# Layer 0 gate and up projection: seven block products for eight on four channel tiles, in a written instruction order

## The chip, the core and the metric

One of the eight cores of a Trainium2 chip runs the whole program: TensorE (PE; its weight loads are listed as PEld), VectorE (DVE), ScalarE (ACT), GpSimd (POOL) and SyncE (SP), which issues the DMAs. The metric is the device time of one execution in microseconds. The kernel before took 3100.1 us (median of 3 runs, 3099.51 to 3101.63).

## What is computed

Two layers of a backbone over 256 latent tokens (`h`) and 256 context tokens (`hc`), 2048 channels, fp32 throughout. Layer 0 mixes tokens by pooling, layer 1 by neighbourhood attention, and each is followed by a gated MLP with 5504 hidden channels. The part that the change touches is the MLP of layer 0, for both streams, and the modulation vectors of layer 1, which are computed beside it:

```python
def conv_ffn(u, w_gate, w_up, conv_w, conv_b, w_down):
    T = u.shape[1]
    gp = jnp.pad(u @ w_gate, ((0, 0), (1, 1), (0, 0)))
    gte = gp[:, :T] * conv_w[0] + gp[:, 1:T + 1] * conv_w[1] + gp[:, 2:] * conv_w[2] + conv_b
    return (jax.nn.silu(gte) * (u @ w_up)) @ w_down
...
ml = (silu_c @ w_mod[i] + b_mod[i]).reshape(B, 6, 1, D)
...
h = h + ml[:, 5] * conv_ffn(modulate(rms_norm(h, norm2_g[i]), ml[:, 3], ml[:, 4]),
                            ffn_w_gate[i], ffn_w_up[i], ffn_conv_w[i], ffn_conv_b[i], ffn_w_down[i])
...
hc = hc + mc[5] * conv_ffn(modulate(rms_norm(hc, norm2_g[i]), mc[3], mc[4]), ...)
```

## The kernel before, in words

Channels lie on the 128 partitions, so 2048 channels are 16 channel tiles (`KT`), and the 5504 hidden channels are 43 hidden tiles `f` (`NF`). The normalised input of the MLP stands in 16 tiles `A[k]`, each `[128, 2, 2, 256]`: first index high and low part, second the stream (latent, context), third the token. Every fp32 number is split into a high part that TensorE multiplies in one pass (type fp32r) and the rest, its low part; a product is three matmuls (weight high by input high, weight high by input low, weight low by input high), accumulated in a PSUM bank.

`load` fetches weights in pieces of 128 x 1024 (512 KB), `split` makes the two halves: ScalarE copies the high part (line 143), VectorE subtracts it to give the low part (line 145). In the MLP of layer 0 the pairs of high and low tiles come from four buffers in turn (three of the pool `whp`, one of `whx`), each 1024 columns wide.

- `gu0(f)` computes gate and up for hidden tile `f`: for each of the two, 16 channel tiles by three matmuls over 512 columns (both streams side by side), lines 631 to 633, so 96 matmuls per hidden tile. The first eight hidden tiles come from another place (`partial`, before the stage).
- `gate0` makes the activation of a hidden tile: the centred convolution (lines 364, 366, 368), SiLU (371), the product with up (372) and the split into high and low (378, 379).
- `down0(c, ...)` takes a chunk of four hidden tiles to the 16 output tiles (`mg`, `m`): lines 657 to 659, 12 matmuls for one output tile, 192 for a chunk of four. Of every chunk but the last ScalarE multiplies the bank by the modulation gate (line 669, two streams) and GpSimd adds the result to `hl` or `hc` (line 670). For the last chunk VectorE does both in one operation from PSUM (line 663).
- `mod_pairs` computes the modulation of layer 1 beside this on VectorE: for pieces of `wmod`, fetched into a ring of three staging buffers two steps ahead, a multiply-add by a scalar into `macc` (lines 239 and 241), at the end of a vector a transposition and a sum (251, 252), a small matmul (`quarter_sum`) and the bias (181). It is a generator, `pump`: each `next(pump)` is one piece, and calls in `gu0` and `down0` place them.

The order of the whole program is set by a scheduler over the instructions of all engines; it may move instructions of one engine past each other. Staging buffers (`wst`) are three for weights and three for the modulation in this stage.

## Time and profile before

| | |
|---|---|
| median of 3 runs | 3100.1 us |
| the profiled execution | 3103.48 us, of which its span 3101.7 us |
| PE busy | 3030.0 us (98%), 15082 instructions |
| DVE busy | 1932.6 us (62%), 2748 instructions |
| ACT busy | 1373.2 us (44%), 2219 instructions |
| POOL busy | 826.1 us (27%), 823 instructions |
| chain that ended last | PE 94% |

The stage of the MLP of layer 0 with full hidden tiles lies between about 520 and 1710 us of the span. Times of the profile are counted from the span's start. A line such as "L631 PE MATMUL g<-A,wg" names line, engine, operation, what is written and what is read. Matmuls are pipelined: a matmul over 512 columns is listed with some 390 ns, and the next one starts long before it ends, so that the cost of one is the distance from start to start.

### The profile page before, as it was taken

How to read it: one execution, taken by the hardware profiler on the slowest of the kernel's cores; microseconds unless marked ns; L12 is line 12 of the kernel's file. 1: busy time of each engine (PE TensorE's matmuls, PEld its weight loads, DVE VectorE, ACT ScalarE, POOL GpSimd, SP SyncE). 2: the span in 40 equal slices, each digit the busy share in tenths (PEclk: the TensorE clock that was granted, in tenths of full speed). 3: DMA queues.
4: the chain of work that ended last, by engine and by line, in shares of the span. 5: the costliest groups of instructions: out<-in, count | busy, mean ns of one | idle time of the engine just before them, and what ended most of it. 6: DMA issues, size and time to landing. Idle time of an engine off the chain costs nothing.

```text
span 3101.7 us, 40819 instructions
## 1 busy us (share of the span) xinstructions
PE 3030.0 (98%) x15082; PEld 2414.3 (78%) x15082; DVE 1932.6 (62%) x2748; ACT 1373.2 (44%) x2219; POOL 826.1 (27%) x823
## 2 busy tenths in 40 slices
PE   6999899999999999999999999999999999999998
PEld 2565558888888888888888788878788888888887
DVE  4445674285765848567485665564777666666666
ACT  3333454333233332323334444343545666656665
POOL 2011213213031230302213000000002466556665
PEclk9999999999999999999999999999999999999999
DMA  9978573264846657475573333332345565555563
GB/s 376 333 271 306 177 246 102 89 217 149 251 141 206 198 162 247 133 225 171 182 226 118 102 113 106 102 114 96 111 153 179 177 196 188 192 189 185 179 195 117
DMA packets 177927, 559.70 MB, mean 180 GB/s; under 512 B 17600, under 2 KB 22208, under 8 KB 177728
## 3 DMA queue, kind: packets, MB, share of 16 engines
q1 hardware_dynamic: 177728, 557.10, 55.0%
q8 instruction: 119, 1.95, 0.3%
q14 instruction: 80, 0.66, 0.1%
HBM read 554.93 MB, written 2.10 MB: 180 GB/s over the span
## 4 chain that ended last, share of the span: by engine, by line
PE 94%; DMA 2%; DVE 2%; POOL 1%; ACT 1%; issue 0%; SPq 0%; DVEq 0%; ACTq 0%; POOLq 0%
PE g L766 5%; PE u L766 5%; PE d L657 5%; PE d L659 5%; PE d L658 5%; PE d L813 4%; PE u L631 4%; PE u L632 4%; PE u L633 4%; PE g L631 4%; PE g L633 4%; PE g L632 4%; PE mod L193 3%; PE u L769 3%; PE g L769 3%; PE d L817 2%
## 5 line engine op out<-in xcount | busy, mean ns | idle before, releaser
L670 POOL TENSOR_TENSOR hl<-hl,dy 128x256 f32<-128x256 f32 x160 | 149.0, 931 | 958.6 <-ACT dy L669 957.3
L828 POOL TENSOR_TENSOR hl<-hl,dy 128x256 f32<-128x256 f32 x320 | 331.5, 1069 | 188.4 <-ACT dy L826 186.1
L241 DVE SCALAR_TENSOR_TENSOR macc<-wm,sc,macc 128x512 f32<-128x512 f32 (+1 forms) x360 | 325.2, 935 | 68.6 <-DMA wm<-wmod 67.6
L669 ACT ACTIVATE dy<-d,modT 128x256 f32<-128x256 f32 x320 | 133.5, 470 | 196.8 <-PE d L659 195.5
L193 PE MATMUL mod<-wm,sc 128*32 128x512 f32 x768 | 134.6, 618 | 26.6 <-DMA wm<-wmod 26.5
L670 POOL TENSOR_TENSOR hc<-hc,dy 128x256 f32<-128x256 f32 x160 | 126.0, 787 | 0.0
L145 DVE TENSOR_TENSOR wd_2l<-wd,wd_2h 128x1024 fp32r<-128x1024 f32 (+1 forms) x44 | 53.9, 1229 | 112.8 <-ACT wd_2h L143 112.8
L826 ACT ACTIVATE dy<-d,modT 128x512 f32<-128x512 f32 x160 | 104.4, 683 | 42.7 <-PE d L817 41.2
L915 POOL TENSOR_TENSOR rk<-rk,rp 128x256 f32<-128x256 f32 x16 | 13.2, 826 | 365.4 <-DVE rk L914 309.8
L145 DVE TENSOR_TENSOR wd_3l<-wd,wd_3h 128x1024 fp32r<-128x1024 f32 (+1 forms) x44 | 52.0, 1202 | 80.6 <-ACT wd_3h L143 80.6
L145 DVE TENSOR_TENSOR wd_1l<-wd,wd_1h 128x1024 fp32r<-128x1024 f32 (+1 forms) x44 | 53.7, 1224 | 58.6 <-ACT wd_1h L143 58.6
L466 POOL TENSOR_TENSOR pf<-ws,inv 128x256 f32<-128x256 f32 x32 | 27.7, 886 | 222.4 <-DVE ws L461 154.7
L193 PEld LDWEIGHTS mod<-wm,sc 128*32 128x32 f32 x768 | 23.6, 110 | 81.0 <-issue 59.4
L143 ACT CAST wd_1h<-wd 128x1024 fp32r<-128x1024 f32 (+1 forms) x44 | 45.2, 1029 | 79.8 <-PE u L632 50.6
L145 DVE TENSOR_TENSOR wd_0l<-wd,wd_0h 128x1024 fp32r<-128x1024 f32 (+1 forms) x44 | 54.6, 1247 | 40.7 <-ACT wd_0h L143 40.6
L1004 ACT ACTIVATE sb<-sb,nm 128x512 f32<-128x512 f32 x64 | 46.1, 721 | 64.4 <-DVE nm L1000 63.2
L143 ACT CAST wd_0h<-wd 128x1024 fp32r<-128x1024 f32 (+1 forms) x44 | 45.3, 1031 | 57.9 <-PE u L766 29.1
L792 DVE TENSOR_TENSOR actb<-sgb,actb 128x256 fp32r<-128x256 f32 x43 | 52.3, 1216 | 27.0 <-ACT actb L791 27.0
L657 PE MATMUL d<-act,wd_2h 128*128 128x512 f32 x172 | 68.0, 395 | 0.0
L658 PE MATMUL d<-act,wd_2h 128*128 128x512 f32 x172 | 67.9, 395 | 0.0
L657 PE MATMUL d<-act,wd_3h 128*128 128x512 f32 x172 | 67.9, 395 | 0.0
L657 PE MATMUL d<-act,wd_0h 128*128 128x512 f32 x172 | 67.9, 395 | 0.0
(1752 smaller groups left out, 9286.1 us busy)
## 6 DMA issues: line engine op xcount, KB each, us to landing
wm<-wmod SPq DMA_DIRECT2D x384, 512.0 KB, 6.1
wd<-wd SPq DMA_DIRECT2D x168, 512.0 KB, 4.4
wg<-wg SPq DMA_DIRECT2D x156, 512.0 KB, 4.6
wu<-wu SPq DMA_DIRECT2D x156, 512.0 KB, 4.5
wv<-wv SPq DMA_DIRECT2D x32, 512.0 KB, 3.9
wk<-wq SPq DMA_DIRECT2D x32, 512.0 KB, 4.0
wq<-wq SPq DMA_DIRECT2D x32, 512.0 KB, 3.7
wo<-wo SPq DMA_DIRECT2D x32, 512.0 KB, 4.4
```

The lines of the kernel that those rows point to most:

```text
L145: eng.tensor_tensor(lo[:, :n], t[:, :n], hi[:, :n].bitcast(F32), op=ALU.subtract)
L193: nc.tensor.matmul(ps[32 * j : 32 * j + 32, :], sc[:, 4 * g + j, :], ts[j // 2][0][:, 512 * (j % 2) : 512 * (j % 2) + 512], start=(g == 0) ...
L241: nc.vector.scalar_tensor_tensor(acc[s], v, sc2[:, k, s : s + 1], acc[s], op0=ALU.mult, op1=ALU.add)
L631: nc.tensor.matmul(ps, hi[:, c : c + P], xh, start=(k == 0), stop=False)
L632: nc.tensor.matmul(ps, hi[:, c : c + P], xl, start=False, stop=False)
L633: nc.tensor.matmul(ps, lo[:, c : c + P], xh, start=False, stop=(k == KT - 1))
L657: nc.tensor.matmul(ps, hi[:, o : o + P], xh, start=(i == 0), stop=False)
L658: nc.tensor.matmul(ps, hi[:, o : o + P], xl, start=False, stop=False)
L670: nc.gpsimd.tensor_tensor(h_of(s)[:, k, :], h_of(s)[:, k, :], y[:, s], op=ALU.add)
L766: nc.tensor.matmul(ps, hi[:, c : c + P], flat(B[k]), start=(k == 0), stop=False)
L769: nc.tensor.matmul(ps[:, T:], lo[:, c : c + P], B[k][:, 0], start=False, stop=(k == KT - 1))
L828: nc.gpsimd.tensor_tensor(hl[:, k, :], hl[:, k, :], y[:, q], op=ALU.add)
```

## The change

From the second chunk (`down(1)`) to the last gate and up (hidden tile 42), the stage is written as a list of `works` (matmul groups), `units` (splits of a weight, now 512 columns of high and 512 of low in one buffer), `loads` and `gates` (small steps of an activation), and emitted in that order inside `tc.manual_schedule`, which leaves the instructions of the five engines in the order written. The last chunk is still done by `down0`, under the scheduler.

Channel tiles 0 to 3 of gate and up are done by Strassen's method: the two streams by two halves of the four channel tiles form one 2 x 2 block matrix, the two halves by gate and up the other, and seven products of 256 columns (two channel tiles each) take the place of eight. Sums of the inputs (`sums`) are made once; sums of the weights (`first`, `second`) and of the products (`lacks`) are made by GpSimd in each hidden tile, and VectorE adds them to the banks (`fix`). The result of a chunk's down projection is added to the streams by VectorE alone, straight from PSUM. The chunks become `runs` (the third has three hidden tiles, the last four). The modulation gives up control after each half of a piece, and says how long it took, and the loop calls it by a running account (`due`) that grows by 0.40 of the matmul time.

```diff
-            for k, v in loaded[i]:
+            for j, (k, v) in enumerate(loaded[i]):
+                if j:
+                    yield 1.6
...
+            yield 1.4 if m == 2 else 1.6
...
-            yield
-        ending()
...
+    runs = [[*range(4)], [*range(4, 8)], [8, 9, 10]] + [list(range(f, f + 4)) for f in range(11, NF, 4)]
...
-        extra.append(whx)
...
-                if c > 1:
-                    next(pump, None)
...
+        J = 2
+        JC = P * J
...
+        NR = NW // 2
+        SLOTS = 7
+        def half(v, n, name):
...
+            hi, lo = t[:, :n], t[:, 512 : 512 + n]
+            nc.scalar.copy(hi, v)
+            nc.vector.tensor_tensor(lo, v, hi.bitcast(F32), op=ALU.subtract)
...
+            def fix():
+                for ps, e in ((b1, e1), (b2, e2)):
+                    nc.vector.tensor_tensor(ps, ps, flat(e), op=ALU.add)
...
+            def first():
+                b11, b12, b22 = x.t[:, :JC], y.t[:, :JC], y.t[:, JC : 2 * JC]
+                z = box["z"] = whx.tile([P, 2 * JC], F32, tag="z", bufs=2, name=nm + "z")
+                nc.gpsimd.tensor_tensor(z[:, :JC], b12, b11, op=ALU.subtract)
+                nc.gpsimd.tensor_tensor(b12, b22, b12, op=ALU.subtract)
+                nc.gpsimd.tensor_tensor(z[:, JC:], b22, z[:, :JC], op=ALU.subtract)
+
+            def second():
+                nc.gpsimd.tensor_tensor(x.t[:, :JC], x.t[:, JC : 2 * JC], box["z"][:, JC:], op=ALU.subtract)
...
+                        nc.tensor.matmul(ps, hi[:, c : c + P], xh, start=(own and i == 0), stop=False)
+                        nc.tensor.matmul(ps, hi[:, c : c + P], xl, start=False, stop=False)
+                        nc.tensor.matmul(ps, lo[:, c : c + P], xh, start=False, stop=(own and i == J - 1))
...
+            def lacks():
+
+                e1, e2 = box["e1s"], box["e2s"]
+                nc.gpsimd.tensor_tensor(e2[:, 0], e2[:, 0], e1[:, 0], op=ALU.add)
+                nc.gpsimd.tensor_tensor(e1[:, 1], e1[:, 1], e2[:, 0], op=ALU.add)
+                nc.gpsimd.tensor_tensor(e2[:, 0], e2[:, 0], e2[:, 1], op=ALU.add)
+                nc.gpsimd.tensor_tensor(e2[:, 1], e2[:, 1], e1[:, 1], op=ALU.add)
...
+            wide, small = 0.69, 0.35
+            work([g1], wide * R, others(g1, "b1", 2 * J, R, True, False), [g1])
+            work([u1], wide * R, others(u1, "b2", 2 * J, R, True, False), [u1])
+            work([w0], small * J, product(1, w0, 0, "e1", 0))
+            work([w0], small * J, product(2, w0, 1, "b1", 0), [w0])
+            work([w1], small * J, product(7, w1, 0, "e1", 1), [], out("e1"))
+            work([w1], small * J, product(3, w1, 1, "b2", 0), [w1])
+            work([w2], small * J, product(6, w2, 1, "e2", 0))
+            work([w2], small * J, product(5, w2, 0, "e2", 1), [w2], out("e2"))
+            work([w3], small * J, product(4, w3, 0, "b1", 1), [w3])
+            work([g2], 4 * wide, others(g2, "b1", 8, 4, False, False), [g2], lacks)
...
+                    def end(m=m, mg=mg, ps_=ps_):
+                        k = 4 * mg + m
+                        for s in both:
+                            nc.vector.scalar_tensor_tensor(h_of(s)[:, k, :], ps_[m][:, T * s : T * s + T], M(0, 5, k, s),
+                                                           h_of(s)[:, k, :], op0=ALU.mult, op1=ALU.add)
...
+        gates.extend(sums(0) + sums(1))
+        down(1)
+        for c, fs in enumerate(runs):
+            for i, f in enumerate(fs):
+                if f > NS:
+                    tile0(f)
+                    if i == 0 and c > 2:
+                        down(c - 1)
+
+        with tc.manual_schedule(engines={mybir.EngineType.PE, mybir.EngineType.Activation, mybir.EngineType.DVE,
+                                         mybir.EngineType.Pool, mybir.EngineType.SP}):
...
+                if started:
+                    due = min(due + 0.40 * us, 6.0)
+                if more_:
+                    for _ in range(2):
+                        if due > 0:
+                            due -= next(pump, 1.0e9)
```

What this does to the order. On PE, at the start of hidden tile 20, the kernel before has (`g0_20` is the bank, `A0_0_3` channel tile 0):

```order
L631 MATMUL g0_20_6868<-A0_0_3_2896,wg0_20h0_6839 128x512
L632 MATMUL g0_20_6868<-A0_0_3_2896,wg0_20h0_6839 128x512
L633 MATMUL g0_20_6868<-A0_0_3_2896,wg0_20l0_6840 128x512
L631 MATMUL g0_20_6868<-A1_0_3_2936,wg0_20h0_6839 128x512
L632 MATMUL g0_20_6868<-A1_0_3_2936,wg0_20h0_6839 128x512
```

and the change, after 24 such matmuls on channel tiles 4 to 7 (`e1` is a bank of its own, `b1` that of the gate, `s3` an input sum):

```order
L886 MATMUL w0_20_b1_7679<-A2_0_3_2985,w0_20_b1_7590 128x256
L887 MATMUL w0_20_b1_7679<-A2_0_3_2985,w0_20_b1_7590 128x256
L888 MATMUL w0_20_b1_7679<-A2_0_3_2985,w0_20_b1_7590 128x256
L886 MATMUL w0_20_b1_7679<-A3_0_3_3048,w0_20_b1_7590 128x256
L887 MATMUL w0_20_b1_7679<-A3_0_3_3048,w0_20_b1_7590 128x256
L888 MATMUL w0_20_b1_7679<-A3_0_3_3048,w0_20_b1_7590 128x256
L886 MATMUL w0_20_e1_7729<-s3_0_4120,w0_20_b2_7651 128x256
L887 MATMUL w0_20_e1_7729<-s3_0_4120,w0_20_b2_7651 128x256
L888 MATMUL w0_20_e1_7729<-s3_0_4120,w0_20_b2_7651 128x256
```

The 24 matmuls of 512 columns on channel tiles 0 to 3 are gone; 42 of 256 columns stand there.

On DVE, in the first quarter of a down projection (chunk or run 5), the kernel before has splits of weights and one activation, no adding to the streams:

```order
L145 TENSOR_TENSOR wd0_5_0l0_8467<-wd0_5_0_0_8462,wd0_5_0h0_8466 128x1024
L145 TENSOR_TENSOR wd0_5_0l1_8471<-wd0_5_0_1024_8464,wd0_5_0h1_8470 128x1024
L366 SCALAR_TENSOR_TENSOR g1_27_8452<-g0_27_8333,vt_70,g1_27_8452 128x2x255
L368 SCALAR_TENSOR_TENSOR g1_27_8452<-g0_27_8333,vt_70,g1_27_8452 128x2x255
L145 TENSOR_TENSOR wd0_5_1l0_8557<-wd0_5_1_0_8552,wd0_5_1h0_8556 128x1024
```

and the change (`macc` is the modulation, `hl` and `hc` the streams, `w0_23` and `act_23` hidden tile 23):

```order
L252 SCALAR_TENSOR_TENSOR macc_1_3_8103<-wm1_3_5_8319,sc2_81,macc_1_3_8103 128x512 x2
L804 SCALAR_TENSOR_TENSOR g1_23_8493<-w0_23_b1_8279,vt_70,g1_23_8493 128x2x255
L806 SCALAR_TENSOR_TENSOR g1_23_8493<-w0_23_b1_8279,vt_70,g1_23_8493 128x2x255
L947 SCALAR_TENSOR_TENSOR hl_84<-d0_5_0_0_8489,modT0_20_3075,hl_84 128x256
L947 SCALAR_TENSOR_TENSOR hc_91<-d0_5_0_0_8489,modT0_20_3075,hc_91 128x256
L814 TENSOR_TENSOR sg_23_8503<-sg_23_8503,w0_23_b2_8301 128x512
L252 SCALAR_TENSOR_TENSOR macc_1_3_8103<-wm1_3_5_8319,sc2_81,macc_1_3_8103 128x512 x2
L822 TENSOR_TENSOR act_23_8517<-sg_23_8503,act_23_8517 128x512
L947 SCALAR_TENSOR_TENSOR hl_84<-d0_5_0_1_8513,modT0_20_3075,hl_84 128x256
L947 SCALAR_TENSOR_TENSOR hc_91<-d0_5_0_1_8513,modT0_20_3075,hc_91 128x256
```

Modulation, activation and the adding to the streams now stand in one queue between the splits.

On POOL the adds to the streams are gone from these runs, and each hidden tile has eight sums, four of weights (lines 838 to 843, with the next tile's ahead) and four of products (900 to 903):

```order
L843 TENSOR_TENSOR w0_20_x_7480<-w0_20_x_7480,w0_20_z_7569 128x256
L838 TENSOR_TENSOR w0_21_z_7750<-w0_21_y_7695,w0_21_x_7669 128x256
L839 TENSOR_TENSOR w0_21_y_7695<-w0_21_y_7695 128x256
L840 TENSOR_TENSOR w0_21_z_7750<-w0_21_y_7695,w0_21_z_7750 128x256
L900 TENSOR_TENSOR w0_20_e2s_7784<-w0_20_e2s_7784,w0_20_e1s_7760 128x256
L901 TENSOR_TENSOR w0_20_e1s_7760<-w0_20_e1s_7760,w0_20_e2s_7784 128x256
L902 TENSOR_TENSOR w0_20_e2s_7784<-w0_20_e2s_7784 128x256
L903 TENSOR_TENSOR w0_20_e2s_7784<-w0_20_e2s_7784,w0_20_e1s_7760 128x256
```

Over the written part this makes, on DVE, 446 splits of 512 columns and 34 of 256, 288 adds to the streams of 128 x 256, 68 `fix` adds of 128 x 512, and the unchanged activations and modulation; on POOL 272 sums for the 34 hidden tiles and 12 for the inputs (four of 512 columns, eight of 256).

## Rows read from the trace of the kernel before

**Rows 1.** The page: the chain that ended last, by engine.

```profile
PE 94%; DMA 2%; DVE 2%; POOL 1%; ACT 1%; issue 0%; SPq 0%; DVEq 0%; ACTq 0%; POOLq 0%
```

**Rows 2.** Busy us by stretch: length, PE, PEld, DVE, ACT, POOL, then PE clock, DMA share, GB/s.

```profile
520.00:1650.00 1130.00, 1130.00 (x4942) 925.25 (x4941) 716.62 (x884) 388.80 (x582) 228.74 (x275) 1.00 0.59 185
2380.00:3060.00 680.00, 680.00 (x3894) 597.21 (x3893) 454.27 (x461) 419.58 (x612) 410.73 (x339) 1.00 0.58 188
```

**Rows 3.** Line 631, gate matmuls: duration ns min/median/max, first and last start us.

```profile
L631 PE MATMUL g<-A,wg_9h x16: 389/389/397, 521.2 to 531.4; 128*128 128x512 f32 x16
...
L631 PE MATMUL g<-A,wg_11h x16: 389/389/389, 565.1 to 575.3; 128*128 128x512 f32 x16
```

**Rows 4.** Timeline of PE (start us, us): a down projection's first matmul, and two gate stretches.

```profile
852.59 0.40 PE L657 MATMUL d<-act,wd_0h 128*128 128x512 f32 x1
...
897.12 0.40 PE L631 MATMUL g<-A,wg_20h 128*128 128x512 f32 x1
...
899.66 0.39 PE L631 MATMUL g<-A,wg_20h 128*128 128x512 f32 x1
...
908.29 0.40 PE L633 MATMUL g<-A,wg_20l 128*128 128x512 f32 x1
```

**Rows 5.** Timeline of PE in layer 1's last chunk: 256 columns, 36 matmuls apart.

```profile
3069.60 0.28 PE L809 MATMUL d<-actb,wd_0h 128*128 128x256 f32 x1
...
3073.92 0.28 PE L809 MATMUL d<-actb,wd_1h 128*128 128x256 f32 x1
```

**Rows 6.** Line 809, its weight loads: duration ns min/median/max.

```profile
L809 PEld LDWEIGHTS d<-actb,wd_0h x12: 192/192/192, 3069.5 to 3073.4; 128*128 128x128 f32 x12
```

**Rows 7.** Groups by line and shape, 520 to 1650 us: count | busy us, mean ns | idle before.

```profile
L241 DVE SCALAR_TENSOR_TENSOR macc<-wm,sc,macc 128x512 f32<-128x512 f32 x240 | 171.3, 761 | 0.2
L241 DVE SCALAR_TENSOR_TENSOR macc<-wm,sc,macc 128x1024 f32<-128x1024 f32 x120 | 153.9, 1282 | 68.4 <-DMA wm<-wmod 67.6
L366 DVE SCALAR_TENSOR_TENSOR g<-g,vt,g 128x510 f32<-128x510 f32 x35 | 26.1, 745 | 0.5
L372 DVE TENSOR_TENSOR sg<-sg,u 128x512 f32<-128x512 f32 x35 | 23.9, 683 | 34.4 <-PE u L633 33.6 <-ACT sg L371 0.8
L251 DVE STREAM_TRANSPOSE modu<-macc 128x512 f32<-128x512 f32 x30 | 19.5, 688 | 0.0
L252 DVE TENSOR_REDUCE modr<-modu 128x16 f32<-128x512 f32 x30 | 18.6, 660 | 0.0
L239 DVE TENSOR_SCALAR macc<-wm,sc 128x512 f32<-128x512 f32 x16 | 8.9, 598 | 0.0
L143 ACT CAST wd_0h<-wd 128x1024 fp32r<-128x1024 f32 x18 | 18.9, 1051 | 27.3 <-PE g L632 27.3
```

**Rows 8.** Lines 379, 663, 670 and 792: duration ns min/median/max.

```profile
L379 DVE TENSOR_TENSOR act<-sg,act x43: 678/685/1270, 420.9 to 1635.4; 128x512 fp32r<-128x512 f32 x43
L663 DVE SCALAR_TENSOR_TENSOR hl<-d,modT,hl x16: 474/482/485, 1675.8 to 1707.5; 128x256 f32<-128x256 f32 x16
L670 POOL TENSOR_TENSOR hl<-hl,dy x160: 729/738/1682, 480.7 to 1674.4; 128x256 f32<-128x256 f32 x160
L792 DVE TENSOR_TENSOR actb<-sgb,actb x43: 418/427/2432, 2388.5 to 3057.0; 128x256 fp32r<-128x256 f32 x43
```

**Rows 9.** Timeline: two operations back to back on DVE; a DVE and a POOL operation at once.

```profile
1024.70 1.40 DVE L241 SCALAR_TENSOR_TENSOR macc<-wm,sc,macc 128x512 f32<-128x512 f32 x2
...
864.84 1.23 DVE L145 TENSOR_TENSOR wd_2l<-wd,wd_2h 128x1024 fp32r<-128x1024 f32 x1 [0.18 <-ACT wd_2h L143]
...
865.32 1.34 POOL L670 TENSOR_TENSOR hl<-hl,dy 128x256 f32<-128x256 f32 x1 [2.08 <-ACT dy L669]
```

**Rows 10.** Groups of POOL, 2380 to 3060 us.

```profile
L828 POOL TENSOR_TENSOR hl<-hl,dy 128x256 f32<-128x256 f32 x298 | 310.4, 1075 | 188.4 <-ACT dy L826 186.1
L145 POOL TENSOR_TENSOR wu_10l<-wu,wu_10h 128x1024 fp32r<-128x1024 f32 x1 | 2.6, 2602 | 0.0
```

**Rows 11.** DMA issues, 520 to 1650 us: count, size, median us to landing.

```profile
wm<-wmod SPq DMA_DIRECT2D x189, 512.0 KB, 5.7
```

238 lines of the change are left out of this document (214 added, 24 removed).

## The prediction

> **What bounds the kernel now.** I read the chain that ended last first: 94% of the span is TensorE [rows 1]. The busy times by stretch then tell how tight it is where the change works: from 520 to 1650 us PE is busy for 1130.00 of 1130.00 us at full clock, while VectorE works 716.62 us, ScalarE 388.80 and GpSimd 228.74 [rows 2]. So in this stage nothing can be won from a wait of PE, only from fewer or cheaper matmuls, and every wait that the change brings to PE is lost. The questions are what a matmul costs, and whether the other engines, above all VectorE, still keep ahead.
>
> **What PE saves.** Two hidden tiles take 565.1 - 521.2 = 43.9 us [rows 3]: 96 matmuls of 512 columns in 21.95 us, 0.2286 us each. The change takes away 24 of them in each of 34 hidden tiles (9 to 42), 24 x 0.2286 = 5.49 us, and puts in 42 of 256 columns (seven products, two channel tiles, three terms). Matmuls of that shape stand back to back in layer 1's last chunk with the same high, high, low pattern: 36 of them from 3069.60 to 3073.92, 0.120 us each [rows 5]. 42 x 0.120 = 5.04 us. The saving is 0.45 us in a hidden tile, **15.3 us** in 34. The seven products for eight should give an eighth of 5.49, 0.69; a third of that goes to the part of a matmul that does not shrink with its columns. One thing could add to the saving: a stretch of gate matmuls runs at (908.29 - 899.66) / 38 = 0.2272 us [rows 4], against the mean of 0.2286; if the other 72 matmuls of a tile all ran so, 72 x 0.0014 x 34 = 3.4 us more. I leave that in the range.
>
> The Trainium skill, "TensorE: Matmul & The Clock Gate" (section "Wait — 56ns, not 53.3ns?"), gives the distance of warm matmuls as columns over 2.4 GHz plus some 2.5 ns. By it, as an estimate, 512 columns are 215.8 ns and 256 are 109.2, and the saving would be (24 x 0.2158 - 42 x 0.1092) x 34 = 20.2 us. The rows of this kernel show 228.6 and 120 ns, so the trace disagrees and I keep 15.3.
>
> The down projections keep their 192 matmuls: 897.12 - 852.59 = 44.53 us [rows 4], a run of three 33.4. The written part is thus 34 x 21.50 + 8 x 44.53 + 33.4 = 1121 us of PE.
>
> **What VectorE must do in these 1121 us.** Modulation as before: 171.3 + 153.9 + 19.5 + 18.6 + 8.9 = 372 us [rows 7]. Splits: 446 of 512 columns at 0.685, the same operation in line 379, and 34 of 256 at 0.427, that of line 792 [rows 8]: 320. Adding to the streams: 288 x 0.482, line 663 [rows 8]: 139. `fix`: 68 x 0.683, as line 372, also one operand from PSUM [rows 7]: 46. Convolutions 68 x 0.745, products 34 x 0.683, low parts 34 x 0.685: 97. Together 974 us, 87%. That is an upper count: two operations of 0.761 back to back take 1.40, not 1.52 [rows 9], some 0.1 us less for each; over 1408 operations 140 us, which leaves 834, 74%. Before it was 716.62 of 1130, 63%. So VectorE is not the bound by its work alone, but the cover shrinks from 37% to between 13 and 26%. ScalarE gains more small copies and loses the scaling of the down results; at 34% before it has room.
>
> **What is late next.** Costs that I put on PE:
> - *The head, 3 us (0 to 9).* The input sums are 12 operations of GpSimd, eight of 0.738 and four of 512 columns, which lie between 0.738 and 2.6 [rows 8, 10], say 1.4: 11.5 us from the start of `down(1)`. The copies that wait for them stand on ScalarE, and their low parts on VectorE, ahead of the split of the fourth piece of the second quarter (`mg` 1), which PE needs after 48 + 9 matmuls, 13.2 us. With the copy and the low part (some 1.2 us) that comes 0 to 2 us late; each sum that has to wait for VectorE as in rows 9 (1.34 against 0.738, 0.6 us) adds to it.
> - *The two down projections under the scheduler, 1.5 us (0 to 14).* Without the fourth buffer (`extra`), the second half of a quarter's weights can be split only when the quarter before is done: 1.05 for the copy [rows 7] and 1.23 for the low part [rows 9]. At six such places PE has the first half of the weights for three output tiles to do, 17 matmuls, 3.9 us. Hidden if the queues are short; 6 x 2.3 = 14 if not.
> - *The quarters of the written down projections, 2.5 us (0 to 36).* Of seven slots four are held until the last output tile of a quarter. The fourth piece of the next quarter is split after the first group of that tile and needed six groups (18 matmuls, 4.2 us) later; copy and low part take 1.2, so VectorE may be 3.0 us behind. What stands before it there are one or two modulation steps (1.40 us each [rows 9]) and the adding of a tile, 0.96 us. Between hidden tiles the slots reach over 10 us ahead, so nothing is lost there.
> - *The end, nothing.* The activation of hidden tile 42 now lies right before the last down projection. Its chain on VectorE and ScalarE is some 7 us, and PE has 36 matmuls of hidden tiles 39 to 41 to do first, 8.3 us. If that cover fails, under 2 us.
>
> Sum: the profiled execution took 3103.48 us. 3103.5 - 15.3 + 7 = 3095.2. It lies 3.4 above the median of the runs, so on that scale **3092**; with a part of the faster matmul distance I take **3091**, 9 us or 0.3% less. A difference under 0.2%, 6.2 us, is what a measurement of this kernel hardly tells from none.
>
> **The rivals.**
> *VectorE becomes the bound, through GpSimd (slower).* In rows 9 a sum on GpSimd that starts while VectorE subtracts two operands from SBUF takes 1.34 us instead of 0.738: it waited. The other way round it is VectorE that waits: line 792 in layer 1 takes 0.418 us at best and 2.432 at worst [rows 8], with GpSimd busy 410.73 of 680 us there [rows 2]. Splits and modulation have both operands in SBUF as these do. If each sum held VectorE up for its full length, that is 272 x 0.738 + 11.5 = 212 us: 834 + 212 = 1046, still under 1121, but 974 + 212 = 1186, 65 over. It decides from a loss of (1121 - 974) / 272 = 0.54 us for each sum, with no overlap of VectorE's operations. Half of the excess, 33 us, gives 3103.5 - 15.3 + 33 - 3.4 = **3118**. The Trainium skill says so too, "SBUF — State Buffer", section "Who interferes with whom": a VectorE instruction with two SBUF inputs and a GpSimd instruction that reads SBUF exclude each other, and the one that starts second waits for the whole of the first. By that rule, with which these rows agree, every sum here meets VectorE's splits and modulation so. For it: VectorE's queue holds such operations two thirds of the time. Against it: the sums of a tile fall where its queue is short (in the last four splits), and back-to-back operations do overlap.
> *The gain is given back in the down projections (no change).* `macc` waited 67.6 us for its transfers before [rows 7], which take 5.7 us each [rows 11] and are fetched two steps ahead; now such a wait stands in front of splits and of the adding to the streams. If one boundary of quarters in four shows PE a step of 1.40 us, that is 9 x 1.40 = 12.6 us in place of 2.5: 3091 + 10 = **3101**.
> *The products cost more than a matmul (the change doesn't do what it says).* A weight load takes 0.192 us [rows 6]; if they no longer overlapped, 42 x 0.192 = 8.06 against 5.49, 87 us more over 34 tiles: some **3190**. Rows 5 speak against it: with the same loads the distance is 0.120.
>
> **How the numbers follow.** Forecast 0.60, given back 0.22, VectorE the bound 0.15, loads 0.03. The forecast's own range is 3081 (no cost, all matmuls at 0.2272) to 3096; some 0.04 of its chance lies within 0.2% of before, which is above 3093.9. The range from 3082 to 3108 leaves out the loads and most of the VectorE case, 0.17. Faster 0.56; within 0.2% 0.04 + 0.18, and 0.03 of a mild VectorE case, 0.25; slower 0.04 of "given back" worse than its middle, 0.12 and 0.03: 0.19.
>
> **What would show it.** Right: hidden tiles of 21.4 to 21.6 us on PE with products at 0.120, PE still above 99% busy in the written part, its only idle time some 3 us in the second quarter of `down(1)`, and VectorE between 75 and 93% busy. VectorE as bound: PE idle before groups that wait for a low part, in hidden tiles too, with VectorE near 100% and splits well over 0.685. Given back: PE idle of about 1 us at quarters of down projections alone. The forecast is wrong if the products stand over 0.125 apart, or if PE is idle for more than 12 us in the written part.

## The result, and the profile after

The changed kernel took 3105.77 us (median of 20 runs, 3102.94 to 3112.78), the kernel before 3100.77 beside it (20 runs): a ratio of 1.0017, interval 1.001 to 1.0023. It is 5.0 us slower, where 9 us less was forecast. The time lies within the range that was given (3082 to 3108), but the kernel became slower where it was to become faster.

The page of the changed kernel, busy time by engine and the chain that ended last (before: [rows 1]):

```profile
PE 3022.5 (97%) x15694; PEld 2437.1 (78%) x15694; DVE 2222.8 (72%) x3382; ACT 1356.2 (44%) x2277; POOL 877.0 (28%) x819
...
PE 78%; DVE 11%; DMA 5%; issue 3%; POOL 2%; ACT 1%; SPq 0%; DVEq 0%; ACTq 0%; POOLq 0%
```

TensorE has less to do than before, and yet 11% of the chain is now VectorE. Busy time by stretch (columns as in [rows 2]):

```profile
520.00:1650.00 1130.00, 1115.39 (x5507) 940.00 (x5506) 992.35 (x1503) 371.96 (x647) 288.17 (x283) 0.99 0.58 182
...
1020.80:1066.60 45.80, 45.00 (x194) 36.14 (x194) 43.26 (x83) 11.36 (x19) 2.92 (x4) 1.00 0.54 168
1066.60:1152.60 86.00, 86.00 (x460) 74.38 (x459) 73.20 (x93) 31.99 (x57) 30.88 (x28) 1.00 0.65 202
...
1164.00:1167.00 3.00, 3.00 (x8) 2.36 (x8) 2.85 (x12) 0.62 (x1) 0.00 (x0) 0.51 0.04 15
```

PE stood idle for 14.6 of the 1130 us, where it had not stood at all [rows 2], and VectorE went from 716.62 us to 992.35. The second row is a down projection: VectorE is busy for 43.26 of 45.80 us, 94% (90 to 96% in the seven projections of four tiles). The third is the four hidden tiles behind it: 85% (84 to 88% in the seven such groups), and PE never waits. Where does PE lose its time, then? Its timeline, through one hidden tile and the projection behind it:

```profile
1131.13 0.39 PE L867 MATMUL w_b<-A,w_g 128*128 128x512 f32 x1
...
1136.58 0.29 PE L886 MATMUL w_e<-A,w_b 128*128 128x256 f32 x1
...
1141.59 0.39 PE L867 MATMUL w_b<-A,w_g 128*128 128x512 f32 x1
...
1152.58 0.39 PE L940 MATMUL d<-act,wd_0p 128*128 128x512 f32 x1
...
1158.36 0.40 PE L942 MATMUL d<-act,wd_3p 128*128 128x512 f32 x1
1163.51 0.47 PE L940 MATMUL d<-act,wd_0p 128*128 128x512 f32 x1 [4.75 <-DVE hc L947]
...
1164.48 0.63 PE L940 MATMUL d<-act,wd_1p 128*128 128x512 f32 x1
1164.91 0.63 PE L941 MATMUL d<-act,wd_1p 128*128 128x512 f32 x1
...
1204.19 0.40 PE L867 MATMUL w_b<-A,w_g 128*128 128x512 f32 x1
```

The tile takes 21.45 us: 42 products in 5.01 us, 0.119 apart, and 72 wide matmuls at 0.227 to 0.229. That is the forecast (21.50). The projection takes 1204.19 - 1152.58 = 51.6 us where [rows 4] had 44.53. At the third output tile of its first quarter, after 24 matmuls, PE waits 4.75 us for a bank that VectorE has not emptied (line 947 adds a bank to the streams). From 1164.06 on the matmuls stand 0.43 us apart for 3 us: the granted clock is 0.51 there (last row of the fence before), the lower level of 1.2 GHz. All waits of PE for another engine between 470 and 1710 us (total, times, longest):

```profile
PE d L940 <- DVE hc L947: 7.8, 4, 4.8
PE d L940 <- ACT wd_3p L761: 4.2, 1, 4.2
PE d L942 <- DVE wd_3p L762: 2.6, 4, 1.1
```

All lie in down projections. From the first matmul of each to the first of the next tile, the eleven projections (nine written, two under the scheduler) sum to 504.6 us; in the run below that has almost no such waits (floor_no_corrections, 0.9 us) it is 483.4, and the 34 hidden tiles take 732.0 us in both. So the projections cost 21.2 us: 7.6 at the head (the first written one), 13.6 in the eight behind it. Without them the kernel would be 16 us faster than before; with them it is 5 slower.

What VectorE did while PE waited, with GpSimd beside it:

```profile
1147.68 0.69 DVE L762 TENSOR_TENSOR wd_0p<-wd,wd_0p 128x512 fp32r<-128x512 f32 x1 [1.21 <-ACT wd_0p L761]
1148.29 1.23 DVE L822 TENSOR_TENSOR act<-sg,act 128x512 fp32r<-128x512 f32 x1
1149.44 2.37 DVE L252 SCALAR_TENSOR_TENSOR macc<-wm,sc,macc 128x512 f32<-128x512 f32 x2
1151.73 1.22 DVE L762 TENSOR_TENSOR wd_1p<-wd,wd_1p 128x512 fp32r<-128x512 f32 x1
1152.88 0.68 DVE L762 TENSOR_TENSOR wd_2p<-wd,wd_2p 128x512 fp32r<-128x512 f32 x1
...
1154.08 1.40 DVE L252 SCALAR_TENSOR_TENSOR macc<-wm,sc,macc 128x512 f32<-128x512 f32 x2
...
1158.54 0.69 DVE L795 TENSOR_TENSOR w_b<-w_b,w_e1s 128x512 f32<-128x512 f32 x1
...
1162.50 0.47 DVE L947 SCALAR_TENSOR_TENSOR hl<-d,modT,hl 128x256 f32<-128x256 f32 x1
1162.89 0.47 DVE L947 SCALAR_TENSOR_TENSOR hc<-d,modT,hc 128x256 f32<-128x256 f32 x1
```

```profile
1148.21 0.76 POOL L900 TENSOR_TENSOR w_e2s<-w_e2s,w_e1s 128x256 f32<-128x256 f32 x1 [13.61 <-ACT w_e2s L894]
...
1151.34 1.07 POOL L903 TENSOR_TENSOR w_e2s<-w_e2s,w_e1s 128x256 f32<-128x256 f32 x1
```

The first output tile's 12 matmuls are through near 1155.4; the sum that empties its bank starts at 1162.50. In between VectorE never rests. From 1147.68 on its queue holds the splits of the first quarter and of three pieces of the second, four modulation steps (two operations each), and the fix (line 795) and convolution of the hidden tile before. And three rows of it are long: the low part takes 1.23 us for 0.68, the two operations of a modulation step 2.37 for 1.40, a split 1.22 for 0.68, just while GpSimd does the four sums of the corrections (1148.2 to 1152.4).

A late drain alone does not make PE wait. In the projection at 1020.84 us the first output tile's bank was emptied at 1030.8, 4.3 us after the third output tile had begun (1026.50), and PE had not waited: four banks go round (`bank` in the kernel). At 1155 us small sums of the modulation (`modt`) took two of the four, and they stood in them until VectorE, late as it was, read them behind the drain. PE, then VectorE:

```profile
1155.37 0.29 PE L165 MATMUL modt_14s<-modr,quad 128*128 128x16 f32 x2
1155.51 0.37 PE L165 MATMUL modt_15s<-modr,quad 128*128 128x16 f32 x2
...
1163.94 0.67 DVE L181 TENSOR_TENSOR modT<-modt_14s,vt 32x4 f32<-32x4 f32 x4
```

So the third output tile needed the first one's bank. All 7.8 us of waits for a bank fall while such sums hold one or two of the four, and so do 42.1 of the 42.5 us of such waits in the ten runs below that have them, act_pool_sums and double_sums apart. No run moved these sums alone, so what they cost by themselves is not shown.

The head is another queue. GpSimd (first fence), ScalarE (second):

```profile
521.35 1.19 POOL L680 TENSOR_TENSOR hc<-hc,dy 128x256 f32<-128x256 f32 x1
522.50 3.55 POOL L720 TENSOR_TENSOR v<-A 128x512 f32<-128x512 f32 x2
...
535.09 0.72 POOL L731 TENSOR_TENSOR z<-v,x 128x256 f32<-128x256 f32 x1
```

```profile
534.48 0.62 ACT L734 CAST s<-x 128x512 fp32r<-128x512 f32 x1 [4.06 <-POOL x L726]
...
536.15 0.61 ACT L761 CAST wd_3p<-wd 128x512 fp32r<-128x512 f32 x1
```

GpSimd still adds the projection before until 522.50, then needs 13.3 us for the input sums; ScalarE stands 4.06 us before their copies, with the copy of the fourth piece (`wd_3p`, 536.15) behind them, which PE wanted at 532.5.

### The profile page after: what moved, and what is told of

Read it like the earlier page. It is cut to its first block, busy times and chain, and to the rows that moved or that the text cites. A ratio compares the mean times of both kernels' runs of the same rounds, so it can differ in the third digit from the quotient of the medians.

```text
span 3106.2 us, 42536 instructions
## 1 busy us (share of the span) xinstructions
PE 3022.5 (97%) x15694; PEld 2437.1 (78%) x15694; DVE 2222.8 (72%) x3382; ACT 1356.2 (44%) x2277; POOL 877.0 (28%) x819
## 4 chain that ended last, share of the span: by engine, by line
PE 78%; DVE 11%; DMA 5%; issue 3%; POOL 2%; ACT 1%; SPq 0%; DVEq 0%; ACTq 0%; POOLq 0%
PE g L1079 5%; PE u L1079 5%; PE d L1126 4%; DMA wm<-wmod 4%; DVE macc L252 3%; PE mod L193 3%; PE d L942 3%; PE d L940 3%; PE w_b L867 3%; PE w_b L869 3%; PE w_b L868 3%; PE d L941 3%; PE u L1082 3%; PE g L1082 3%; PE d L1130 2%
## 5 line engine op out<-in xcount | busy, mean ns | idle before, releaser
L252 DVE SCALAR_TENSOR_TENSOR macc<-wm,sc,macc 128x512 f32<-128x512 f32 (+1 forms) x360 | 352.0, 1008 | 46.4 <-DMA wm<-wmod 45.2
L1141 POOL TENSOR_TENSOR hl<-hl,dy 128x256 f32<-128x256 f32 x320 | 331.8, 1070 | 188.3 <-ACT dy L1139 186.0
L838 POOL TENSOR_TENSOR w_z<-w_y,w_x 128x256 f32<-128x256 f32 x34 | 30.5, 896 | 640.7 <-DMA w_y<-wu 568.3
L867 PE MATMUL w_b<-A,w_u 128*128 128x512 f32 x408 | 160.1, 392 | 0.0
L867 PE MATMUL w_b<-A,w_g 128*128 128x512 f32 x408 | 159.6, 391 | 0.0
L869 PE MATMUL w_b<-A,w_u 128*128 128x512 f32 x408 | 159.5, 391 | 0.0
L868 PE MATMUL w_b<-A,w_u 128*128 128x512 f32 x408 | 159.4, 391 | 0.0
L869 PE MATMUL w_b<-A,w_g 128*128 128x512 f32 x408 | 159.3, 391 | 0.0
L868 PE MATMUL w_b<-A,w_g 128*128 128x512 f32 x408 | 159.2, 390 | 0.0
L869 PEld LDWEIGHTS w_b<-A,w_u 128*128 128x128 f32 x408 | 76.7, 188 | 16.7
L868 PEld LDWEIGHTS w_b<-A,w_u 128*128 128x128 f32 x408 | 76.8, 188 | 16.4
L869 PEld LDWEIGHTS w_b<-A,w_g 128*128 128x128 f32 x408 | 76.6, 188 | 16.4
L867 PEld LDWEIGHTS w_b<-A,w_u 128*128 128x128 f32 x408 | 76.6, 188 | 16.2
L868 PEld LDWEIGHTS w_b<-A,w_g 128*128 128x128 f32 x408 | 76.7, 188 | 14.9
L867 PEld LDWEIGHTS w_b<-A,w_g 128*128 128x128 f32 x408 | 76.7, 188 | 14.9
L947 DVE SCALAR_TENSOR_TENSOR hl<-d,modT,hl 128x256 f32<-128x256 f32 x144 | 69.2, 480 | 24.6 <-PE d L942 24.4
L761 ACT CAST wd_3p<-wd 128x512 fp32r<-128x512 f32 x32 | 19.8, 620 | 144.7 <-PE d L942 144.7
```

Of the source, the lines that this page charges most:

```text
L252: nc.vector.scalar_tensor_tensor(acc[s], v, sc2[:, k, s : s + 1], acc[s], op0=ALU.mult, op1=ALU.add)
L867: nc.tensor.matmul(box[b], hi[:, c : c + P], xh, start=(start and i == 0), stop=False)
L868: nc.tensor.matmul(box[b], hi[:, c : c + P], xl, start=False, stop=False)
L869: nc.tensor.matmul(box[b], lo[:, c : c + P], xh, start=False, stop=(stop and i == n - 1))
L1141: nc.gpsimd.tensor_tensor(hl[:, k, :], hl[:, k, :], y[:, q], op=ALU.add)
```

## Experiments

Theories as the expectations name them. **A**: VectorE's queue in a projection's first quarter is too long. **B**: GpSimd's sums take VectorE's time. **C**: the fourth piece's slots and loads. **D**: VectorE is loaded to its limit over a projection, so what moves within it is given back. **E**: the written order itself. Sum of the eleven projections, and the hold-up: what VectorE's operations between 640 and 1650 us took beyond the lower quartile of their own line and shape (counted from 8% on), summed from each trace. A blank means that it was not summed. "To before" is the difference of the medians within one set of runs.

| kernel | median us | to before | ratio, interval | projections us | hold-up us |
|---|---|---|---|---|---|
| changed kernel | 3105.8 | +5.0 | 1.0017 (1.001 to 1.0023) | 504.6 | 80.9 |
| late_mod | 3101.7 | -0.1 | 0.9999 (0.999 to 1.0007) | 496.9 | |
| slow_sums | 3098.0 | -3.8 | 0.9988 (0.9979 to 0.9997) | 494.3 | |
| late_gates | 3098.4 | -3.5 | 0.9987 (0.9978 to 0.9996) | 493.2 | |
| act_pool_sums | 3126.0 | +24.1 | 1.008 (1.0067 to 1.0094) | 521.2 | 156.6 |
| all_three | 3101.4 | -0.8 | 0.9999 (0.999 to 1.0008) | 496.2 | 81.7 |
| no_products | 3101.1 | -1.2 | 0.9998 (0.9989 to 1.0007) | 481.0 | 0.4 |
| no_corrections | 3094.7 | -7.6 | 0.9977 (0.9968 to 0.9986) | 490.0 | 23.0 |
| two_edits | 3092.1 | -8.7 | 0.9971 (0.996 to 0.9981) | 488.6 | 80.9 |
| dve_corrections | 3107.2 | +6.4 | 1.0019 (1.001 to 1.0028) | 503.3 | 24.8 |
| dve_corr_two_edits | 3096.7 | -4.1 | 0.999 (0.9981 to 0.9998) | 494.4 | 22.8 |
| double_sums | 3175.6 | +74.8 | 1.0242 (1.0228 to 1.0256) | 566.7 | 116.8 |
| fix_held_too | 3099.2 | -1.2 | 0.9996 (0.9987 to 1.0005) | 495.9 | 80.4 |
| light_projections | 3097.9 | -4.6 | 0.999 (0.9981 to 1.0) | 483.5 | 70.7 |
| floor_no_corrections | 3086.3 | -16.2 | 0.9948 (0.9935 to 0.996) | 483.4 | 21.9 |
| light_spaced | 3088.0 | -13.6 | 0.9952 (0.9938 to 0.9965) | 484.2 | 71.7 |

### Three loads on the queue, one at a time: late_mod, slow_sums, late_gates

late_mod (also no step at u2 and u3 of the tile ahead, cap 9.0 for 6.0):

```diff
-    end if i == n - 1 else None, i == n - 1 and m < 2 and c > 1)
+    end if i == n - 1 else None, i == n - 1 and m < 2 and c > 1 and mg > 0)
```

slow_sums (`head`: the number of works of `down(1)`), then late_gates (`held`: the works of each first quarter):

```diff
-    if gates and gate_due >= 0.6:
+    if gates and gate_due >= (2.7 if at < head else 0.6):
```

```diff
-    if gates and gate_due >= 0.6:
+    if gates and at not in held and gate_due >= 0.6:
```

> Edit: no modulation half step between the last up works of the tile ahead of a down projection and the end of that projection's first quarter; the held half steps follow in the other quarters (the cap on what is owed goes from 6 to 9), so the number of them in the written part stays the same. Theory A (VectorE's queue in a projection's first quarter is too long, so the sums that empty the d banks come 5 to 7 us late): three to five half steps of 1.4 us leave that stretch, the waits of TensorE for a d bank (7.8 us) and the slow clock behind them go, the seven four-tile projections fall from a mean of 46.8 us to 44.6 to 45.5, time 3105.8 - 10 to 15 = 3091 to 3096. Theory B (VectorE is late there because GpSimd's weight sums hold it up, 2.37 us for 1.40): the steps that are held up are then others, at most 3 us gained, 3102 to 3106. Theory C (the projection's fourth piece comes late through slots and loads, not VectorE): no change, 3105 to 3107.

> Edit: in the first written projection (down(1)) the ten steps of the input sums are taken one in about 2.8 us of TensorE work, not one in each 0.69 us. Theory A (the sums of GpSimd, ScalarE and VectorE in the second quarter hold up the fourth piece's split): the wait of 4.3 us at 532 us, the 0.8 us behind it and the slow clock after them go, the projection falls from 52.25 to 45 to 47 us, time 3105.8 - 5 to 7 = 3099 to 3101. Theory C (the fourth piece is late because its slot comes free only with the last output tile of the quarter before): the wait stays near 4 us whatever the sums do, time 3104 to 3107.

> Edit: the gate steps of the tile ahead of a four-tile projection are held back until the projection's first quarter is over; the modulation stays where it is. Theory A: 1.38 (fix) + 1.5 (conv2) + 0.7 + 0.7 = 4.3 us of VectorE's queue leave the first quarter, the sums that empty the d banks come about 3 us earlier, the longest wait (4.9 us) falls to 1 to 2 us, time 3105.8 - 5 to 10 = 3096 to 3101. Theories B and C: at most 2 us, 3104 to 3106.

late_mod gained 5.1 us (difference of the two columns "to before") where 10 to 15 were expected: the seven projections of four tiles came to 44.6 to 46.2 us (44.6 to 51.6 as changed), but the held steps came back: the run of three tiles rose from 35.4 to 38.2 us, and the head stayed as it was. slow_sums: the wait at 532 us is gone and the first written projection fell by 7.6 us, which settles the head for A against C; the gain is 8.8 us, somewhat more than expected. late_gates: the longest wait for a bank fell to 2.2 us, and the gain of 8.5 us is in the upper half of what was expected.

### The drains back on ScalarE and GpSimd: act_pool_sums

```diff
-    nc.vector.scalar_tensor_tensor(h_of(s)[:, k, :], ps_[m][...], M(0, 5, k, s), h_of(s)[:, k, :], ...)
+    y = f0.tile([P, 2, T], F32, tag="t2", name=f"dy{c}_{k}")
+    nc.scalar.activation(y[:, s], ps_[m][...], AF.Copy, scale=M(0, 5, k, s))
+    nc.gpsimd.tensor_tensor(h_of(s)[:, k, :], h_of(s)[:, k, :], y[:, s], op=ALU.add)
```

> Edit: the sums of the written projections on the streams go back to ScalarE (scale) and GpSimd (add), as in the kernel before; all else as changed. Theory A: VectorE loses 32 x 0.40 = 13 us of each four-tile projection's 44.5 and the d banks no longer wait for its queue; ScalarE, at 44% busy, takes them: time 3105.8 - 8 to 15 = 3091 to 3098. Theory B (GpSimd holds up VectorE): 32 more GpSimd adds in each projection slow VectorE further, splits come late, time 3108 to 3125. Theory C: 3104 to 3108.

B's number, and more. Waits of PE between 640 and 1680 us, then a row of ScalarE's timeline:

```profile
PE d L940 <- ACT dy L948: 9.6, 3, 6.0
PE d L942 <- DVE wd_3p L762: 6.0, 6, 1.4
PE d L940 <- DVE modT L181: 4.4, 2, 2.9
```

```profile
1170.29 0.62 ACT L761 CAST wd_2p<-wd 128x512 fp32r<-128x512 f32 x1 [5.69 <-DMA wd<-wd]
```

Two causes. ScalarE empties banks in the order of its queue: in front of the drain at 1176.96 us, for which PE waited 6.0 us, stood a copy of a weight that waited 5.69 us for its transfer, and two steps of an activation that waited 2.10 and 2.64 us for VectorE. And VectorE gained less than it lost work: 256 sums, 122 us, left it between 640 and 1650 us, but its hold-up grew by 76 us. So adding the down sums on VectorE, a part of the change, is right in this kernel.

### All three edits, and the products left out: all_three, no_products, no_corrections

all_three is the three diffs above together. no_products (the other six products, `sums` and `fix` go too; up alike), then no_corrections (all four lines of `lacks`):

```diff
-    work([w0], small * J, product(1, w0, 0, "e1", 0))
+    for j in range(4):
+        work([g[j]], 4 * wide, others(g[j], "b1", 4 * j, 4, j == 0, j == 3), [g[j]])
```

```diff
-    nc.gpsimd.tensor_tensor(e2[:, 0], e2[:, 0], e1[:, 0], op=ALU.add)
```

> Edit: the edits of late_mod, slow_sums and late_gates together. Each of them alone moved the end of the stage from 1710.9 to about 1702.7 us in the profile. Theory A (one queue, three loads on it): the first projection falls to about 45 us (52.25 as changed), the seven others to 44.6 to 45.4, so 7 + 15 = 22 us at most and about 17 after what the three share: end of the stage 1689 to 1696, time 3085 to 3091, ratio to before 0.995 to 0.997. Theory D (what was held up comes back at another place, since VectorE is busy for 85 to 92% of the written part): tiles grow above 86.5 us for four, or later quarters wait; time 3093 to 3100.

> Edit: the written order, the sums on the streams by VectorE and the modulation in half steps stay; the seven products, their weight sums, input sums and the two corrections go, each tile is 96 wide matmuls again. Theory A: a tile takes 96 x 0.2286 = 21.95 us, 34 of them 15.3 us more than as changed; the projections lose the input sums (7.7 us at the head), the fix (1.4 us of VectorE a tile) and GpSimd's sums, so that of 25.6 us of excess some 5 remain; time 3105.8 + 15.3 - 20 = 3098 to 3104, near the kernel before. Theory E (the order itself is what costs: every projection stands behind a tile's end, products or not): the projections keep 15 us and more of their excess, time 3110 to 3116.

> Leaves out: the four sums of GpSimd by which e1 and e2 become the corrections of a tile (the uncorrected banks are added in their place). Theory B (GpSimd on VectorE's way): these sums run just when a tile ends, 1148.2 to 1152.4 us in the profile, and hold up the activations' low part, two modulation steps and two splits by about 0.55, 0.97 and 0.55 us, some 2 us in all at each projection: the drains come 2 us earlier, the waits for a d bank fall from 7.8 us to 2 to 4, the time by 5 to 8 us to 3098 to 3101. Theory A without B (the queue is long whatever GpSimd does): at most 2 us gained, 3104 to 3106.

all_three failed A and came near D, 1.4 us above the range that D gave: the head's wait is gone, but six of the seven four-tile projections stand at 45.8 to 46.5 us, and in the run of three tiles (41.0 us, where 33.4 are needed) the modulation, begun late, came in a bunch: steps of 3.11 and 2.63 us in front of the sums that empty two banks, the second after 1.29 us of waiting for its transfer. no_products came out as A has it: projections without a wait (a mean of 44.7 for seven of four tiles), tiles of 22.0 us, and the time of the kernel before within 0.1%. So E falls: the written order, VectorE's drains and the half steps cost nothing by themselves, with VectorE as lightly loaded as it is there. no_corrections bore out B and more: 12.6 us less than as changed (each taken to before) for 136 sums of GpSimd fewer. In these three kernels the same operation, the low part of an activation, and the modulation (groups by line and shape, 640 to 1650 us); changed kernel:

```profile
L822 DVE TENSOR_TENSOR act<-sg,act 128x512 fp32r<-128x512 f32 x30 | 32.5, 1084 | 0.0
...
L252 DVE SCALAR_TENSOR_TENSOR macc<-wm,sc,macc 128x512 f32<-128x512 f32 x210 | 159.0, 803 | 0.2
```

without products:

```profile
L818 DVE TENSOR_TENSOR act<-sg,act 128x512 fp32r<-128x512 f32 x30 | 20.5, 685 | 0.0
...
L252 DVE SCALAR_TENSOR_TENSOR macc<-wm,sc,macc 128x512 f32<-128x512 f32 x210 | 147.5, 746 | 0.2
```

without corrections:

```profile
L822 DVE TENSOR_TENSOR act<-sg,act 128x512 fp32r<-128x512 f32 x31 | 22.8, 737 | 0.0
...
L252 DVE SCALAR_TENSOR_TENSOR macc<-wm,sc,macc 128x512 f32<-128x512 f32 x210 | 150.6, 763 | 0.2
```

### Load or order: two_edits, dve_corrections, dve_corr_two_edits, double_sums

two_edits is the diffs of slow_sums and late_gates. dve_corrections (four such lines, as a step of the gate ahead of `fix`; dve_corr_two_edits has all of these), then double_sums:

```diff
-    nc.gpsimd.tensor_tensor(e2[:, 0], e2[:, 0], e1[:, 0], op=ALU.add)
+    nc.vector.tensor_tensor(e2[:, 0], e2[:, 0], e1[:, 0], op=ALU.add)
```

```diff
+    spare = f0.tile([P, 2, T], F32, tag="t2", name=nm + "spare")
+    for i in range(4):
+        nc.gpsimd.tensor_tensor(spare[:, i % 2], e2[:, i % 2], e1[:, i // 2], op=ALU.add)
```

> Edit: slow_sums and late_gates together, without late_mod, whose held modulation steps came in a bunch in the later quarters and in the second written projection (40.98 us for 33.4). Theory D (VectorE is loaded to its limit in a projection, and what is moved within it is given back) says that holding gate steps, 4.3 us, is small enough to fit: the head's 7 us and the d-bank waits both go, projections of 44.6 to 46, time 3105.8 - 7.4 - 7.8, about 3091 to 3094, ratio to before 0.996 to 0.9975. If the two edits share what they gain: 3095 to 3098.

> Edit: the four sums of the corrections are done by VectorE, as a step of the gate ahead of the fix, and not by GpSimd. Theory B (what counts is VectorE's time, and GpSimd's sums take it away): 31 tiles x 4 x 0.41 = 51 us of work come to VectorE in the stretch 640 to 1650 us, and the part of the 81 us of hold-up that goes with these sums, some 58 us by no_corrections, leaves it: about even, VectorE busy within 15 us of the 986 us of the changed kernel (sum of durations), time 3099 to 3106. Theory A (the length of the queue in operations counts): one more step of 1.64 us in each first quarter, time 3107 to 3112.

> Edit: dve_corrections and two_edits together. Theory B with D: the corrections on VectorE are held back with the other gate steps, outside the first quarter; the hold-up of splits at a tile's end is gone: 2 to 4 us below two_edits, 3088 to 3092. If VectorE's total load alone counts: the same as two_edits within 2 us.

> Edit: each tile's four correction sums on GpSimd are followed by four more of the same size into a spare tile that nobody reads. VectorE, ScalarE and TensorE get no instruction more. Theory B: the hold-up of VectorE grows by about what no_corrections took away, 58 us, to some 140 us in the stretch 640 to 1650 us; the waits for d banks and splits grow, time 3105.8 + 6 to 20 = 3112 to 3126. Theory A without B: 3104 to 3108.

two_edits took the time that was expected and beats both kernels; the waits for a bank were to go and did so in part (4.4 us, 7.8 as changed). dve_corrections: the hold-up fell by 56 us, 51 us of work came, and the time stayed (+6.4 to before, +5.0 as changed): B's account, in which only VectorE's time counts, holds in sum; the time lies 1 us above B's range, in A's. This run also speaks against a rival to hold-up that the expectations did not name: the corrections delay GpSimd's next weight sum (line 843), for which ScalarE's copies waited 83.5 us as changed and 25.1 in no_corrections (640 to 1650 us). Here that wait fell as well, to 22.8 us, and the time did not fall. Together with two_edits it did not add up (3096.7, expected at most 3092): it is slower than two_edits, so the later place of 51 us is worth no more than hold-up at the tile's end. double_sums cost far more than expected, 75 us to before, with no instruction more on VectorE, ScalarE or TensorE. Its waits, and one of its projections:

```profile
PE d L943 <- DVE hc L950: 19.2, 10, 7.1
PE d L945 <- DVE wd_3p L762: 10.5, 10, 1.9
```

```profile
901.40:954.30 52.90, 46.14 (x193) 35.66 (x192) 50.42 (x88) 12.48 (x21) 10.90 (x11) 1.00 0.52 152
```

The doubled sums run on into the projection (GpSimd 10.90 us there, for 2.9 to 4.1 in the four-tile projections as changed); VectorE is busy for 95% of it, and PE waits 6.8 us of 52.9. The direction is B's; the size, more than three times the most that was expected, is more than the hold-up explains by itself (36 us more up to 1650 us). The clock adds to it: ten stretches at the lower level, some 22 us by the distances of their matmuls. And the edit does more than hold VectorE up: it takes a buffer for the spare tile, and GpSimd comes later with its own weight sums (ScalarE waits 159.5 us for line 843, 83.5 as changed), so that the groups of four hidden tiles take 86.2 to 88.4 us (86.0 to 86.5 as changed). The 75 us are not a price of hold-up alone.

### What two_edits leaves: fix_held_too, light_projections, floor_no_corrections, light_spaced

All on top of two_edits. fix_held_too (`quiet`: works with no modulation step), then light_projections, then what light_spaced adds to it in `mod_pairs`; floor_no_corrections takes away the four lines of `lacks`:

```diff
+    quiet.add(len(works) - 1)
-    held.update(range(len(works), len(works) + 4 * len(runs[c - 1])))
+    held.update(range(len(works) - 1, len(works) + 4 * len(runs[c - 1])))
```

```diff
-    due = min(due + 0.40 * us, 6.0)
+    due = min(due + (0.33 if us == 0.69 else 0.45) * us, 6.0)
```

```diff
+        yield 4.0
+        yield 4.0
         end(0)
```

> Edit: as two_edits, and at the last work of the tile ahead of a four-tile projection neither a gate step (the fix, which two_edits still lets through) nor a modulation step is taken; the fix follows after the first quarter, the modulation step in the projection. Theory A: 1.37 + 1.40 = 2.8 us leave the queue ahead of the first sum on the streams; the waits that two_edits has left (2.5 us with 1.7 us of slow clock behind it at 1147 us, 1.3 us at 1558 us) go, time 3092.1 - 3 to 5.5 = 3086.5 to 3089. Theory D (VectorE's total load in a projection): the step comes back in the later quarters, waits for the fourth piece's split grow; 3091 to 3095.

> Edit: as two_edits, and the modulation is taken at 0.33 us of VectorE for each us of a projection and at 0.45 in the tiles (0.40 in both before), so that the total stays. Theory D (VectorE's load over a projection is the limit): 0.07 x 44.5 = 3.1 us less for VectorE in each projection, the last waits (4.4 us, 1.7 us of slow clock) go, projections of 44.6 to 45.1, tiles unchanged at 86.0 to 86.5 for four, time 3092.1 - 3 to 6 = 3086 to 3089. Theory A (the order of the first quarter's queue alone): there the steps stay as they are, 3091 to 3093. If the tiles are as full as the projections: tiles above 87 us for four, 3094 to 3100.

> Leaves out: GpSimd's four sums for a tile's corrections, as no_corrections; otherwise two_edits. Theory B with D: with 58 us less hold-up and the two edits no projection waits, all at 44.6 to 45.1, and the time is the saving of the products in full with nothing given back: 3092.1 - 5 to 7 = 3085 to 3087. If something else than VectorE (slots, loads) limits the projections: within 2 us of two_edits.

> Edit: as light_projections, and the modulation's last sums come two steps (about 18 us) after its last transposition. Theory D: the two waits of TensorE for modr (8.8 us) and the slow clock behind one of them (1.3 us) go, the projections stay at 44.6 to 45.2 with one of 46.6, time 3097.9 - 8 to 10 = 3088 to 3090, below two_edits (3092.1) and above floor_no_corrections (3086.3). If another wait takes their place: 3091 to 3096.

fix_held_too missed A's gain and came out worse than D's range: 2.8 us less in front of the first drain, and PE waits 5.5 us for the fourth piece's split, six times, where two_edits waited for none. In this case a better order in one place was paid for in another. floor_no_corrections is where it should be: PE waits 0.9 us in all projections, and the time is 16.2 us under before, the products' saving in full. light_projections took nearly all waits out of the projections (1.4 us are left) but met a new one, at the modulation's last sums, and missed the 3086 to 3089 us that D gave (waits of PE, 470 to 1700 us):

```profile
PE modt_22s L165 <- DVE modr L263: 5.2, 1, 5.2
PE modt_23s L165 <- DVE modr L263: 3.6, 1, 3.6
PE d L942 <- DVE wd_2p L762: 1.4, 1, 1.4
```

light_spaced makes these sums two steps later, and then only this is left in the projections:

```profile
PE d L944 <- DVE wd_1p L764: 0.5, 1, 0.5
PE d L944 <- DVE wd_3p L764: 0.3, 1, 0.3
...
1012.10:1057.50 45.40, 45.07 (x195) 36.31 (x194) 43.45 (x78) 11.66 (x19) 3.90 (x5) 1.00 0.66 191
```

At 3088.0 us it is the fastest of those that leave nothing out: 13.6 us under before and some 18 under the kernel as changed. The modulation's share of a four-tile projection (durations over its length) fell from a mean of 0.41 in two_edits to 0.37, in the tiles it rose from 0.40 to 0.43. But VectorE is still busy for 43.45 of 45.40 us of a projection, 96% (last row). That the lighter load is the reason, as theory D has it, is not shown. Another reason stands beside it: in light_projections and light_spaced the modulation's small sums fall into hidden tiles, so that they hold no bank in a projection, and neither run has a wait for a bank.

## Why the prediction was wrong, by its own steps

- *What PE saves*: right. 15.3 us were forecast; tiles of 21.53 us on average (732.0 / 34) against 21.50, products 0.119 apart against 0.120. floor_no_corrections shows the whole saving in the time, 16.2 us.
- *What VectorE must do*: too low. 834 to 974 us in the written part were forecast; it was busy for 992 us of 520 to 1650 alone [compare rows 2]. Some 81 us of that is hold-up by GpSimd, which the sum left out and kept for a rival.
- *The head, 3 us (0 to 9)*: the mechanism was right, the size was not, 7.6 us. The 11.5 us of input sums were counted from the start of `down(1)`; GpSimd began 3.3 us later, behind the sums of the projection before, and took 13.3 us.
- *The two down projections under the scheduler, 1.5 us*: nothing measurable; the last takes 44.66 us.
- *The quarters of the written down projections, 2.5 us (0 to 36)*: **the step that failed**, 13.6 us. The forecast looked only at the fourth piece's split, with one or two modulation steps and a drain in front of it. PE did wait there, but for 2.1 us outside the head. It waited 7.8 us for the banks of output tiles, to which the forecast gave no term; the longest of these waits, 4.75 us, comes at the third output tile of a first quarter. What was overlooked is that the modulation's small sums take up to two of four banks and that VectorE can be 7 us behind by then: the splits of two quarters are let go at once as the tile ahead frees its slots, the last tile's gate steps follow, and GpSimd's corrections fall on just this place. The lower clock behind two of these waits cost some 1.6 us each, which no term had either. That the time still lies in the range is no support for the forecast: the range reached up to 3108 to take in other outcomes.
- *The rivals*: the result is that of "given back in the down projections" (3101, with a chance of 0.22), and 5 us beyond it. Its mechanism, a transfer of modulation weights that holds up VectorE's queue, shows in one projection of the nine, the run of three tiles: VectorE waits 2.42 us for it, right ahead of the sums that empty a bank, and PE 1.47 us for this bank (VectorE's timeline, changed kernel):

```profile
662.56 1.28 DVE L252 SCALAR_TENSOR_TENSOR macc<-wm,sc,macc 128x1024 f32<-128x1024 f32 x1 [2.42 <-DMA wm<-wmod]
```

  In the others VectorE waits for no such transfer. Its queue is long there in part because of the mechanism of the other rival, "VectorE becomes the bound, through GpSimd": 81 us of hold-up over 244 sums, 0.33 us each, against 0.54 named as the point from which VectorE would bound the whole stage. So it makes PE wait in projections (VectorE 90 to 96% busy) and not in the tiles (84 to 88%); the forecast compared VectorE's work with the whole written part, and no average of the two shows that. "The products cost more than a matmul" did not happen.
- *Its own test*: "PE is idle for more than 12 us in the written part" is what came, 14.6 us.

Settled by the runs: the order costs nothing without the products (no_products), GpSimd's corrections cost some 12 us (no_corrections), the places of the input sums and of the gate steps 8 to 9 us each (slow_sums, late_gates), and without these costs the full saving is there (floor_no_corrections). The three overlap: together they are more than the 21.2 us that the projections lose. Open: what a given place in VectorE's queue is worth (fix_held_too lost by a change of order alone), and how much of the waits would go if the modulation's small sums held no bank in a projection.

## What to carry to other kernels

Compare a helper engine's work with the stretch where it is densest, not with the stage: 88% on average was 90 to 96% in the projections, and there little is left to make up for a late start. The share alone does not tell a wait, though: the projection at 1424.48 us, with VectorE 95% busy, had none, so look also at what stands in the queue ahead of the operation that is due. A sum given to GpSimd was not free for VectorE: a 128x256 sum cost it a third of a microsecond on average, 0.48 us for a correction (the 58 us that no_corrections took away, over 120 sums) and 0.19 for the others (23.0 over 124). So it matters where a sum falls. When an order is written by hand, drains that give banks back should not stand behind work that is only due later (late_gates), and who else takes a bank there should be counted; holding back still more of that work cost time again (fix_held_too).
